# A fifth pair of seven products from the fourth gate/up chunk on, and VectorE's order at the ends of chunks, in a two-layer hybrid encoder

## The chip, the cores and the metric

The kernel runs on one core of one Trainium2 chip. The metric is the device time of one execution in microseconds, as the median of several executions. Profiles show one execution on the chip, with times from the start of its span. TensorE is PE in the profile, VectorE is DVE, ScalarE is ACT, GpSimd is POOL, and SyncE, which issues most DMAs, is SP.

## What is computed

The reference is a trunk of two layers (`DEPTH`) over 256 tokens of width 2048. Everything is float32.

```python
def swiglu(h, w_gate, w_up, w_down):
    return (jax.nn.silu(h @ w_gate) * (h @ w_up)) @ w_down

def reference(x, ...):
    for l in range(DEPTH):
        h = rms_norm(x, pre_mix_norm[l])
        m = hybrid_mixer(h, l, ...)
        x = x + rms_norm(m, post_mix_norm[l])
        h = rms_norm(x, pre_ffn_norm[l])
        f = swiglu(h, w_gate[l], w_up[l], w_down[l])
        x = x + rms_norm(f, post_ffn_norm[l])
    return x
```

The change touches `h @ w_gate` and `h @ w_up` only: 256 x 2048 by 2048 x 5632, twice in each layer.

## The kernel before

**Products.** A float32 product is made of three matmuls on operands rounded to a shorter format: the rounded part `hi` and the rest `lo` of both sides give hi·hi, hi·lo and lo·hi, all added in one PSUM bank (`product`, lines 1075 to 1080). The activations are split once. Each weight block of 256 x 512 (128 partitions x 1024 values) is loaded from HBM into a room `raw`, ScalarE writes `hi` (line 306) and VectorE writes `lo = raw - hi` (line 316). TensorE multiplies a 128 x 128 block of activations by 128 x 512 values in one matmul.

**Chunks and pairs.** The 5632 columns of gate and up are cut into 11 chunks of 512, and the 2048 rows into eight pairs `kp` of two 128-row blocks (loop at line 1253). A chunk adds into four banks, gate and up for each of the two token tiles. One pair takes eight block products, 24 matmuls (`eight`, line 1244), or seven, 21 matmuls, by Winograd's form of Strassen's scheme (`seven_products`, lines 1099 to 1114). `gate_sevens` says which pairs of a chunk are "seven" pairs, and `gate_order` in which order the pairs come.

**What a seven pair costs elsewhere.** Its loads go to rooms `G` (the gate block) and `T` (the up block, to which a DMA of POOL's queue adds half of the gate block, line 258). `mixed_weights` then does, on ScalarE and VectorE: the split of `T` into `hi` and `lo` (lines 279 and 280, 1024 values), a subtraction in `T` (line 289, 512), an addition in `G` (line 290, 1024), and the splits of `T` and `G` into `Th` and `Tl` (512 and 1024). The sums of activations for a pair (`pair_sums`, line 1227, and `token_sums`, line 1082) are made once per layer, at the places (chunk, pair) of `FORM_AT`. Four of the seven products are shared between output blocks: they add up in four extra banks `p1`, `p6`, `p7`, `q5` over all seven pairs of the chunk.

**The end of a chunk.** After the chunk's last seven pair, `shared_part` (line 1116) reads the extra banks: ScalarE copies `p1`, and VectorE makes the four **shared additions** (lines 1120 to 1123). After the chunk's last pair come the **last additions** (lines 1288 and 1291, two each, from the chunk's own banks), the silu on ScalarE (line 1289) and the two multiplications to `act` (line 1293). The banks change sides: the extra banks of chunk c are the main banks of chunk c+1, and the main banks of chunk c are the extra banks of chunk c+1 (lines 1254 and 1275). So TensorE can start chunk c+1 only when the shared additions of chunk c have read the extra banks, and can start the first seven pair of chunk c+1 only when the last additions have read the main banks. The transposes of `act` for the down stage run in the last pair of the next chunk (line 1270).

**Who sets the order.** Each engine works through its own queue in order. Weights are asked for `LOOKAHEAD` = 4 blocks ahead (`feed`, line 296; `fetch`, line 218); there are 4 rooms `raw`, 6 each for `hi` and `lo`, 3 for `G`, 4 for `T`. A scheduler orders the instructions on each engine; `tc.issue_after(i)` puts the instructions inside it behind `i` in their engine's order, and is no wait by itself. `behind()` (line 324) puts the next `held[1]` subtractions of line 316 behind the last shared addition. `helped` (line 207) names gate blocks whose `lo` is made by POOL instead of VectorE (line 309): the second and third pair of each chunk from chunk 2 on; the second one also waits for the latest matmul of a seven pair ("the shared port"). `put_away` (line 362) stores a quarter of x (512 KB, SP's queue) at four chunks of each layer (`AWAY_AT`).

Of the kernel before, what the change touches and what calls it, by code (L numbers as in the profile page):

```python
# [9 lines left out]
F32 = mybir.dt.float32  # L10
# [3 lines left out]
ALU = mybir.AluOpType  # L14
# [10 lines left out]
FF = 5632  # L25
CW = 512
# [18 lines left out]
FIRST_ORDER = (0, 1, 3, 2, 7, 4, 6, 5)  # L45
NEXT_SEVEN = (4, 5, 6)
MORE_SEVEN = (2, 3, 4, 5, 6)
MORE_AT = (2, 3, 4, 5, 6, 7, 8, 9)
MORE_ORDER = (0, 2, 1, 3, 4, 5, 6, 7)
FORM_AT = {(0, 1): 4, (0, 2): 6, (0, 5): 5, (1, 3): 2, (1, 5): 3}  # L50
DOWN_SEVEN = ((4, 7, 10, 12, 15, 17, 20), (3, 5, 8, 10, 13, 15, 18))

AFTER = mybir.DependencyInfo(mybir.DependencyClass.Sync, mybir.DependencyReason.DATA)
# [2 lines left out]
LEVEL = 232  # L56
EARLY = 4
LEAD = 6
AWAY_AT = (1, 3, 4, 5)
X_BACK = 12  # L60


# [4 lines left out]
def gate_sevens(c):  # L67

    if c in MORE_AT:
        return MORE_SEVEN  # L70
    return (FIRST_SEVEN, NEXT_SEVEN)[c] if c < 2 else SEVEN


def gate_order(c):

    if c in MORE_AT:
        return MORE_ORDER
    return FIRST_ORDER if c == 0 else tuple(range(KT // 2))
# [89 lines left out]
def kernel(  # L168
# [15 lines left out]
    nc = tc.nc  # L184
# [14 lines left out]
    def four_banks(odd, names):  # L199
        makers = (bank, bank, bank, last_bank) if odd else (acc_bank,) * 4  # L200
        return [make(n) for make, n in zip(makers, names)]


    order, plan, sevens, plain, own = weight_order()
# [1 line left out]

    helped = {}
    for lay in plan:
        for c in range(2, FF // CW):
            for n in (1, 2):  # L210
                helped[lay["gate"][c, gate_order(c)[n]]] = n == 1
    newest_seven = [None]
# [50 lines left out]
    def mixed_weights(i):  # L263

        g, u = raws[i - 1], raws[i]
        hi = wpool.tile([P, 2, CW], F32R, tag="hi", bufs=6, name=f"hi{i}")
        lo = wpool.tile([P, 2, CW], F32R, tag="lo", bufs=6, name=f"lo{i}")
        if i in own:
            th = wpool.tile([P, 2, CW], F32R, tag="hi", bufs=6, name=f"Th{i}")
            tl = wpool.tile([P, 2, CW], F32R, tag="lo", bufs=6, name=f"Tl{i}")  # L270
            th2 = mix_pool[0].tile([P, 2 * (S + P)], F32R, tag="ah", bufs=1, name=f"T2h{i}")[:, 0:CW]
            tl2 = mix_pool[0].tile([P, 2 * (S + P)], F32R, tag="al", bufs=1, name=f"T2l{i}")[:, 0:CW]
        else:
            th = mix_pool[0].tile([P, 3, CW], F32R, tag="Th", bufs=1 if i in plain else 2, name=f"Th{i}")
            tl = mix_pool[0].tile([P, 3, CW], F32R, tag="Tl", bufs=1 if i in plain else 2, name=f"Tl{i}")
            th2, tl2 = th[:, 2, :], tl[:, 2, :]

        def split(h, l, w):
            nc.scalar.activation(h, w, AF.Copy)  # L279
            nc.vector.tensor_tensor(out=l, in0=w, in1=h.bitcast(F32), op=ALU.subtract)  # L280

        if i in plain or i in own:
            with after_rests():
                nc.vector.tensor_tensor(out=u[:, 0, :], in0=g[:, 0, :], in1=u[:, 0, :], op=ALU.add)
        split(hi, lo, u)
        t1, b22 = ((hi[:, k, :], lo[:, k, :]) for k in range(2))
        t3, t4 = ((th[:, k, :], tl[:, k, :]) for k in range(2))
        t2 = u[:, 1, :]
        nc.vector.tensor_tensor(out=t2, in0=t2, in1=u[:, 0, :], op=ALU.subtract)  # L289
        nc.vector.tensor_tensor(out=g, in0=g, in1=t2.unsqueeze(1).to_broadcast([P, 2, CW]), op=ALU.add)  # L290
        split(th2, tl2, t2)
        split(th[:, 0:2, :], tl[:, 0:2, :], g)
        t2 = th2, tl2
        return {"b22": b22, "t1": t1, "t2": t2, "t3": t3, "t4": t4}
# [25 lines left out]

    rests = []
    held = [None, 0]

    def behind():

        if held[1] == 0:
            return nullcontext()
        held[1] -= 1
        return tc.issue_after(held[0].ins)

    def after_rests():

        return tc.issue_after(rests[-1].ins)
# [28 lines left out]
    def put_away(nm, n):  # L362

        if n == 0:
            away.append(kept.tile([P, NT, D], F32, name=f"away_{nm}"))
        t, h = divmod(n, 2)
        with in_turn():
            nc.sync.dma_start(away[-1][:, t, h * D // 2 : (h + 1) * D // 2], xs[t][h])
# [168 lines left out]
    def start(gen, n=1):  # L537
        running.append([clock[0] + n, gen])
# [577 lines left out]
    def shared_part(extra, w):  # L1116

        p1, p6, p7, q5 = extra
        nc.scalar.copy(w[0], p1)
        nc.vector.tensor_tensor(out=w[1], in0=p6, in1=w[0], op=ALU.subtract)  # L1120
        nc.vector.tensor_tensor(out=w[2], in0=p7, in1=w[1], op=ALU.add)  # L1121
        nc.vector.tensor_tensor(out=w[1], in0=q5, in1=w[1], op=ALU.add)
        return nc.vector.tensor_tensor(out=w[3], in0=q5, in1=w[2], op=ALU.add)

    def shared_sign(t, col):
        return ALU.subtract if (t, col) == (1, 0) else ALU.add

    xT = None
    for l in range(L):
# [27 lines left out]
        for kp in LATE_O:  # L1157
            i, j = (plan[l]["o"][c, kp] for c in (2, 3))
# [4 lines left out]
            if kp == O_SEVEN[0]:  # L1163
                extra = four_banks(False, [f"{q}_o{l}" for q in ("p1", "p6", "p7", "q5")])
# [44 lines left out]
        LAST = FF // CW - 1  # L1209
# [24 lines left out]
        def eight(banks, c, kp, toks, first, last):  # L1234
            g, u = weights(plan[l]["gate"][c, kp], LOOKAHEAD), weights(plan[l]["up"][c, kp], LOOKAHEAD)
            for kk in range(2):
                st = xT[2 * kp + kk]
                for t in toks:
                    tick()
                    stat = (st[:, 0, t * P : (t + 1) * P], st[:, 1, t * P : (t + 1) * P])  # L1240
                    two = banks[2 * t : 2 * t + 2]
                    for part, j, n in ((1, 0, 0), (0, 0, 1), (0, 1, 2)):
                        for a, w in zip(two, (g, u)):
                            nc.tensor.matmul(a, stat[part], w[j][:, kk, :], start=first and kk + n == 0, stop=last and kk == 1 and n == 2)  # L1244
# [8 lines left out]
        for c in range(FF // CW):  # L1253
            banks = four_banks(1 - c % 2, [f"c{q}_{l}_{c}" for q in ("11", "12", "21", "22")])
            mine = gate_sevens(c)
            order = gate_order(c)
            if c == 0:
                for t in range(NT):
                    for kp in order[:2]:
                        eight(banks, c, kp, (t,), kp == order[0], False)  # L1260
                order = order[2:]
            extra = None
            for n, kp in enumerate(order):
                if n == 1 and c in AWAY_AT:
                    put_away(f"ffn{l}", AWAY_AT.index(c))
                if (c, n) in FORM_AT:
                    with after_rests():
                        pair_sums(FORM_AT[c, n])
                if c and n == 7:
                    start(turned(c - 1), 4)  # L1270
                if kp not in mine:
                    eight(banks, c, kp, range(NT), kp == 0, kp == order[-1])
                    continue
                if kp == mine[0]:
                    extra = four_banks(c % 2, [f"{q}_{l}_{c}" for q in ("p1", "p6", "p7", "q5")])
                seven(banks, extra, c, kp, kp == mine[0], kp == mine[-1])
                if kp == mine[-1]:
                    w = [pool.tile([P, CW], F32, tag="t2", name=f"w{j}_{l}_{c}") for j in range(4)]
                    held[:] = shared_part(extra, w), 2
            if c == 0:  # L1280
                act.append(act_room(0))
            if c < LAST:
                act.append(act_room(c + 1))
                results[c] = [act[c + 1].rearrange("p k n -> p (k n)")[:, t * CW : (t + 1) * CW] for t in range(NT)]
            else:
                results[c] = [w[0], w[2]]
            for t in range(NT):
                nc.vector.tensor_tensor(out=w[2 * t], in0=banks[2 * t], in1=w[2 * t], op=shared_sign(t, 0))
                nc.scalar.activation(w[2 * t], w[2 * t], AF.Silu, scale=rs[t][:, 0:1])
            for t in range(NT):  # L1290
                nc.vector.tensor_tensor(out=banks[2 * t + 1], in0=banks[2 * t + 1], in1=w[2 * t + 1], op=ALU.add)
            for t in range(NT):
                nc.vector.scalar_tensor_tensor(
                    out=results[c][t], in0=banks[2 * t + 1], scalar=rs[t][:, 0:1], in1=w[2 * t], op0=ALU.mult, op1=ALU.mult
                )
# [11 lines left out]
        for half in range(2):  # L1307
# [48 lines left out]
            for kp in range(nkp - tail):  # L1356
# [10 lines left out]
                if kp == mine[0]:  # L1367
                    extra = four_banks(1 - half, [f"{q}_d{l}_{half}" for q in ("p1", "p6", "p7", "q5")])
# [90 lines left out]
```

## Time and profile before

| what | value |
|---|---|
| median of 3 runs | 2205.46 us (2204.45 to 2209.45) |
| the profiled execution's own time | 2204.04 us |
| its span, first to last instruction | 2202.3 us |
| mean granted TensorE clock | 0.998 |
| TensorE busy with matmuls | 2175.5 us |
| VectorE busy | 1947.0 us |
| ScalarE busy | 1397.5 us |
| GpSimd busy | 245.7 us |
| gate/up, layer 0 (chunks 0 to 10) | 396.15 to 866.42 us of the span |
| gate/up, layer 1 | 1490.81 to 1962.41 us |

The profile's busy time of TensorE counts a matmul from its start to its modelled end, and matmuls overlap, so 99% busy does not say that TensorE issues at its full rate. The better measure used below is the length of a chunk: each chunk has a fixed number of matmuls, so chunks with the same work can be compared. A view by stretches gives, for each stretch of the span, the busy time of each engine with its number of instructions in brackets. A chunk is cut here at the first matmul of line 1244 into its main banks.

### The profile page before, as it was taken

Reading aid. Unit: us, or ns where it says so; the run is one execution under the profiler, and the core shown is the slowest. Engines: PE = TensorE matmul, PEld = TensorE weight load, DVE = VectorE, ACT = ScalarE, POOL = GpSimd, SP = SyncE. Lnnn points to the kernel's source line nnn. Section 1 sums busy time; section 2 is a strip of 40 time slices with the busy share of each in tenths; the row PEclk is TensorE's granted clock in tenths of the full one; section 3 lists DMA queues with packets and bytes.
Section 4 is the critical chain, followed back from the end, with each engine's and each line's share of the span. In section 5 each row is a group of like instructions: output and inputs, shape, how many; then the busy total and the mean of one; then the engine's idle time right before and its main releaser. Section 6 shows DMA issues by size and latency. Waiting matters only on the chain.

```text
span 2202.3 us, 28747 instructions
## 1 busy us (share of the span) xinstructions
PE 2175.5 (99%) x9944; PEld 1782.5 (81%) x9944; DVE 1947.0 (88%) x2651; ACT 1397.5 (63%) x2087; POOL 245.7 (11%) x239
## 2 busy tenths in 40 slices
PE   9999999999999999999999999999999999999998
PEld 7888888777788888888878888887777888888886
DVE  7888658999999999989878886579999999999997
ACT  7666665765666666666665656657556666566664
POOL 1100000022122120000010000000211211200000
PEclk9999999999999999999999999999999999999999
DMA  9545555587787777767465555556878878767673
GB/s 336 177 163 174 190 195 168 187 279 216 235 256 228 223 236 233 241 211 258 146 239 172 189 174 176 190 171 202 266 215 234 263 225 230 235 227 234 205 262 101
DMA packets 140851, 471.49 MB, mean 214 GB/s; under 512 B 16016, under 2 KB 17040, under 8 KB 140192
## 3 DMA queue, kind: packets, MB, share of 16 engines
q1 hardware_dynamic: 121952, 436.03, 57.5%
q0 software_dynamic: 18176, 33.07, 9.0%
q8 instruction: 78, 1.28, 0.2%
q10 hardware_dynamic: 576, 0.54, 0.1%
q14 instruction: 69, 0.57, 0.1%
HBM read 461.19 MB, written 8.39 MB: 213 GB/s over the span
## 4 chain that ended last, share of the span: by engine, by line
PE 84%; DVE 10%; DMA 2%; issue 2%; ACT 1%; DVEq 0%; SPq 0%; ACTq 0%
PE c L1244 15%; PE in L1078 7%; PE in L1080 7%; PE in L1079 7%; PE dn L1340 4%; PE dn L1341 4%; PE dn L1343 4%; PE p L1079 2%; PE p L1080 2%; PE c L1079 2%; PE c L1080 2%; PE c L1078 2%; PE o L563 2%; PE p L1078 2%; PE o L564 2%
## 5 line engine op out<-in xcount | busy, mean ns | idle before, releaser
L316 DVE TENSOR_TENSOR lo<-raw,hi 128x1024 fp32r<-128x1024 f32 x472 | 568.4, 1227 | 99.2 <-ACT hi L306 97.9
L306 ACT ACTIVATE hi<-raw 128x1024 fp32r<-128x1024 f32 x490 | 505.5, 1054 | 108.7 <-DMA raw<-in_weights_in_turn_dram 37.6
L1244 PE MATMUL c<-hi,xF 128*128 128x512 f32 x1248 | 338.5, 392 | 0.9 <-ACT act L1224 0.5
L258 POOL DMA_DIRECT2D T<-in_weights_in_turn_dram x126 | 110.9, 880 | 1466.3 <-DMA T<-in_weights_in_turn_dram 778.1
L1244 PEld LDWEIGHTS c<-hi,xF 128*128 128x128 f32 x1248 | 231.8, 188 | 50.5 <-DVE w L1121 1.3
L1244 PE MATMUL c<-lo,xF 128*128 128x512 f32 x624 | 193.4, 390 | 2.5 <-DVE lo L316 2.5
L279 ACT ACTIVATE Th<-T 128x512 fp32r<-128x512 f32 x126 | 79.0, 627 | 167.3 <-DVE T L289 149.6
L280 DVE TENSOR_TENSOR lo<-T,hi 128x1024 fp32r<-128x1024 f32 x126 | 172.4, 1368 | 2.9 <-ACT hi L279 2.8
L279 ACT ACTIVATE hi<-T 128x1024 fp32r<-128x1024 f32 x126 | 132.4, 1050 | 66.1 <-PE c L1080 51.9
L1340 PE MATMUL dn<-hi,jh 128*128 128x512 f32 x432 | 168.2, 389 | 0.0
L1341 PE MATMUL dn<-lo,jh 128*128 128x512 f32 x432 | 168.1, 389 | 0.0
L279 ACT ACTIVATE Th<-G 128x1024 fp32r<-128x1024 f32 x126 | 133.3, 1058 | 52.1 <-DVE G L290 51.3
L280 DVE TENSOR_TENSOR Tl<-G,Th 128x1024 fp32r<-128x1024 f32 x126 | 158.8, 1260 | 4.2 <-ACT Th L279 4.2
L306 ACT ACTIVATE hi<-G 128x1024 fp32r<-128x1024 f32 x126 | 133.0, 1056 | 43.0 <-DMA G<-in_weights_in_turn_dram 15.7
L290 DVE TENSOR_TENSOR G<-G,T 128x1024 f32<-128x1024 f32 x126 | 153.8, 1220 | 2.2
L1244 PEld LDWEIGHTS c<-lo,xF 128*128 128x128 f32 x624 | 117.1, 188 | 27.6 <-DVE lo L316 3.0
L316 DVE TENSOR_TENSOR lo<-G,hi 128x1024 fp32r<-128x1024 f32 x108 | 131.5, 1218 | 7.9 <-ACT hi L306 7.6
L1343 PE MATMUL dn<-hi,jl 128*128 128x512 f32 x432 | 133.0, 389 | 0.0
L1078 PE MATMUL in<-hi,xT 128*128 128x512 f32 x328 | 131.8, 404 | 0.6 <-ACT hi L883 0.6
L1078 PE MATMUL in<-hi,xI 128*128 128x512 f32 x328 | 131.1, 401 | 0.0
L1079 PE MATMUL in<-lo,xI 128*128 128x512 f32 x328 | 128.0, 390 | 0.3 <-DVE lo L316 0.3
L1080 PE MATMUL in<-hi,xT 128*128 128x512 f32 x328 | 128.3, 392 | 0.0
(485 smaller groups left out, 4955.8 us busy)
## 6 DMA issues: line engine op xcount, KB each, us to landing
raw<-in_weights_in_turn_dram SPq DMA_DIRECT2D x490, 512.0 KB, 4.6
T<-in_weights_in_turn_dram SPq DMA_DIRECT2D x126, 512.0 KB, 5.2
G<-in_weights_in_turn_dram SPq DMA_DIRECT2D x126, 512.0 KB, 5.5
T<-in_weights_in_turn_dram POOLq DMA_DIRECT2D x126, 256.0 KB, 5.8
GU<-in_weights_in_turn_dram SPq DMA_DIRECT2D x32, 512.0 KB, 6.3
V<-in_weights_in_turn_dram SPq DMA_DIRECT2D x8, 512.0 KB, 3.7
away_ffn<-x SPq DMA_DIRECT2D x8, 512.0 KB, 7.5
xd<-away_ffn SPq DMA_DIRECT2D x8, 512.0 KB, 9.3
```

The lines of the kernel that those rows point to most:

```text
L279: nc.scalar.activation(h, w, AF.Copy)
L280: nc.vector.tensor_tensor(out=l, in0=w, in1=h.bitcast(F32), op=ALU.subtract)
L290: nc.vector.tensor_tensor(out=g, in0=g, in1=t2.unsqueeze(1).to_broadcast([P, 2, CW]), op=ALU.add)
L306: nc.scalar.activation(hi, raw, AF.Copy)
L316: rest = nc.vector.tensor_tensor(out=lo, in0=raw, in1=hi.bitcast(F32), op=ALU.subtract)
L1078: nc.tensor.matmul(a, sh, hi, start=first, stop=False, skip_group_check=open_sums[0])
L1079: nc.tensor.matmul(a, sh, lo, start=False, stop=False, skip_group_check=open_sums[0])
L1080: return nc.tensor.matmul(a, sl, hi, start=False, stop=last, skip_group_check=open_sums[0])
L1244: nc.tensor.matmul(a, stat[part], w[j][:, kk, :], start=first and kk + n == 0, stop=last and kk == 1 and n == 2)
L1340: nc.tensor.matmul(accs[c, t], sh, hi[:, kk, :], start=first, stop=False, skip_group_check=open_sums[0])
L1341: nc.tensor.matmul(accs[c, t], sh, lo[:, kk, :], start=False, stop=False, skip_group_check=open_sums[0])
L1343: nc.tensor.matmul(accs[c, t], sl, hi[:, kk, :], start=False, stop=last, skip_group_check=open_sums[0])
```

## The change

Chunk 2 goes from five seven pairs to the four of the ordinary chunks, in the ordinary order 0 to 7; chunks 3 to 9 keep five. The activations' sums for pair 3 are made in chunk 2 instead of chunk 1 (`FORM_AT`), and the first quarter of x is put away in chunk 2 instead of chunk 1. POOL's help (`helped`) begins in chunk 1. In the ends of chunks whose next chunk has a seven pair as its second pair (chunks 2 to 8), three things are put in a row on VectorE: the shared additions, then the subtractions of that second pair's split, then the last additions. At the other ends only one later `lo` subtraction, not two, is put behind the shared additions (two still at the last chunk).

```diff
-MORE_AT = (2, 3, 4, 5, 6, 7, 8, 9)
+MORE_AT = (3, 4, 5, 6, 7, 8, 9)
 MORE_ORDER = (0, 2, 1, 3, 4, 5, 6, 7)
-FORM_AT = {(0, 1): 4, (0, 2): 6, (0, 5): 5, (1, 3): 2, (1, 5): 3}
+FORM_AT = {(0, 1): 4, (0, 2): 6, (0, 5): 5, (1, 3): 2, (2, 4): 3}
...
-AWAY_AT = (1, 3, 4, 5)
+AWAY_AT = (2, 3, 4, 5)
...
     for lay in plan:
-        for c in range(2, FF // CW):
+        for c in range(1, FF // CW):
             for n in (1, 2):
                 helped[lay["gate"][c, gate_order(c)[n]]] = n == 1
...
         def split(h, l, w):
             nc.scalar.activation(h, w, AF.Copy)
-            nc.vector.tensor_tensor(out=l, in0=w, in1=h.bitcast(F32), op=ALU.subtract)
+            with in_row(i):
+                newest_rest[i] = nc.vector.tensor_tensor(out=l, in0=w, in1=h.bitcast(F32), op=ALU.subtract)
...
+    follows, newest_rest = {}, {}
+
+    def in_row(i):
+
+        return tc.issue_after(follows[i].ins) if i in follows else nullcontext()
...
-                    held[:] = shared_part(extra, w), 2
+                    end = shared_part(extra, w)
+                    second = plan[l]["up"][c + 1, gate_order(c + 1)[1]] if c < LAST else None
+                    if second in sevens:
+                        follows[second] = end
+                    else:
+                        held[:] = end, 2 if second is None else 1
...
+            def ending():
+                return tc.issue_after(newest_rest[second].ins) if second in follows else nullcontext()
+
             for t in range(NT):
-                nc.vector.tensor_tensor(out=w[2 * t], in0=banks[2 * t], in1=w[2 * t], op=shared_sign(t, 0))
+                with ending():
+                    nc.vector.tensor_tensor(out=w[2 * t], in0=banks[2 * t], in1=w[2 * t], op=shared_sign(t, 0))
                 nc.scalar.activation(w[2 * t], w[2 * t], AF.Silu, scale=rs[t][:, 0:1])
             for t in range(NT):
-                nc.vector.tensor_tensor(out=banks[2 * t + 1], in0=banks[2 * t + 1], in1=w[2 * t + 1], op=ALU.add)
+                with ending():
+                    nc.vector.tensor_tensor(out=banks[2 * t + 1], in0=banks[2 * t + 1], in1=w[2 * t + 1], op=ALU.add)
```

## The prediction

> **What bounds the kernel now.** I read the page first, then the view by stretches cut at the chunks, then TensorE's waits, then VectorE's and POOL's timelines at the chunk ends where TensorE waits.
>
> ```profile
> span 2202.3 us, 28747 instructions
> PE 2175.5 (99%) x9944; PEld 1782.5 (81%) x9944; DVE 1947.0 (88%) x2651; ACT 1397.5 (63%) x2087; POOL 245.7 (11%) x239
> ```
>
> TensorE looks full, but its matmuls overlap, so what it loses has to be read from the lengths of chunks. Columns: stretch, length, then busy time and count by engine.
>
> ```profile
> core 0: us, PE busy (x) PEld busy (x) DVE busy (x) ACT busy (x) POOL busy (x), PEclk, DMA share, GB/s
> 442.18:486.02 43.84, 43.14 (x192) 34.85 (x190) 42.53 (x59) 25.12 (x30) 8.99 (x6) 1.00 0.92 299
> 486.02:530.73 44.71, 42.96 (x186) 33.67 (x186) 44.24 (x46) 25.99 (x30) 10.59 (x7) 1.00 0.69 207
> 530.73:575.19 44.46, 42.20 (x186) 33.74 (x185) 43.93 (x47) 27.75 (x34) 9.33 (x8) 1.00 0.82 247
> 575.19:618.01 42.82, 41.60 (x187) 33.98 (x185) 42.72 (x46) 26.47 (x31) 9.10 (x7) 1.00 0.78 235
> 618.01:660.00 41.99, 41.34 (x187) 33.98 (x186) 41.73 (x45) 27.73 (x34) 9.15 (x7) 1.00 0.83 248
> ...
> 701.07:742.62 41.55, 41.31 (x187) 33.97 (x186) 40.31 (x45) 26.85 (x32) 9.17 (x7) 1.00 0.81 232
> 742.62:783.64 41.02, 41.02 (x186) 33.99 (x185) 40.56 (x45) 26.61 (x32) 9.21 (x7) 1.00 0.80 230
> ...
> 824.72:866.42 41.70, 41.70 (x190) 34.61 (x189) 40.38 (x44) 27.14 (x35) 4.17 (x3) 1.00 0.62 199
> ...
> 1536.85:1580.84 43.99, 43.19 (x192) 34.84 (x190) 42.53 (x59) 25.03 (x30) 8.99 (x6) 1.00 0.90 295
> 1580.84:1628.48 47.64, 44.64 (x185) 34.81 (x186) 45.60 (x48) 27.07 (x32) 9.62 (x7) 0.96 0.71 210
> 1628.48:1671.50 43.02, 41.94 (x187) 33.82 (x186) 42.33 (x45) 26.69 (x32) 9.41 (x8) 1.00 0.81 239
> 1671.50:1714.35 42.85, 41.62 (x186) 33.98 (x185) 42.75 (x46) 26.48 (x31) 9.02 (x7) 1.00 0.81 238
> 1714.35:1756.33 41.98, 41.33 (x187) 33.98 (x185) 41.72 (x45) 27.71 (x34) 9.70 (x8) 1.00 0.82 250
> ```
>
> These are chunks 1 to 5, 7, 8 and 10 of layer 0, and 1 to 5 of layer 1. Chunk 8, five seven pairs, takes 41.02 with no idle; chunk 10, four, takes 41.70. The three matmuls between them make 0.68, so a matmul is 0.227, and a chunk of three seven pairs would take 42.38. Against these floors chunks 1 to 5 and 7 lose 1.46, 3.69, 3.44, 1.80, 0.97 and 0.53 in layer 0 (11.9), and 1.61, 6.62, 2.00, 1.83 and 0.96 in layer 1 (13.0; its chunk 7 lost nothing). **24.9 us** are lost, beside a VectorE that is busy 43.93 of 44.46. Who ends the waits (layer 0, chunks 1 to 10):
>
> ```profile
> PE p L1079 <- DVE Tl L280: 2.3, 5, 0.8
> PE q L1078 <- DVE act L1293: 1.5, 1, 1.5
> PE p L1078 <- DVE act L1293: 0.9, 1, 0.9
> ```
>
> Idle here starts at a matmul's modelled end, so it is less than the loss. VectorE's splits are late for the last seven pairs, and its last additions free the banks late for the next chunk's first. At the end of chunk 1, VectorE and POOL:
>
> ```profile
> 482.55 2.81 DVE L280 TENSOR_TENSOR lo<-T,hi 128x1024 fp32r<-128x1024 f32 x1
> ...
> 488.82 2.89 DVE L280 TENSOR_TENSOR Tl<-T,Th 128x512 fp32r<-128x512 f32 x1
> ...
> 495.16 1.39 DVE L1293 SCALAR_TENSOR_TENSOR act<-c,rs_ffn,w 128x512 f32<-128x512 f32 x2
> ...
> 479.62 4.67 POOL L309 TENSOR_TENSOR lo<-G,hi 128x1024 fp32r<-128x1024 f32 x1 [3.88 <-ACT ss L1095]
> ...
> 488.33 2.83 POOL L309 TENSOR_TENSOR lo<-raw,hi 128x1024 fp32r<-128x1024 f32 x1 [0.35 <-ACT hi L306]
> ```
>
> And at the end of chunk 6, where nothing is lost:
>
> ```profile
> 693.20 1.22 DVE L316 TENSOR_TENSOR lo<-raw,hi 128x1024 fp32r<-128x1024 f32 x1
> 694.33 0.68 DVE L1120 TENSOR_TENSOR w<-p,w 128x512 f32<-128x512 f32 x1
> ...
> 696.38 0.68 DVE L1123 TENSOR_TENSOR w<-q,w 128x512 f32<-128x512 f32 x1
> 696.98 1.63 DVE L280 TENSOR_TENSOR lo<-T,hi 128x1024 fp32r<-128x1024 f32 x1
> ...
> 706.05 1.36 DVE L316 TENSOR_TENSOR lo<-raw,hi 128x1024 fp32r<-128x1024 f32 x1
> ...
> 695.11 2.41 POOL L309 TENSOR_TENSOR lo<-G,hi 128x1024 fp32r<-128x1024 f32 x1 [4.93 <-PE c L1080]
> ```
>
> From start to start a VectorE instruction of 1024 values holds its queue for 1.13 (693.20 to 694.33), one of 512 for 0.60 (696.38 to 696.98). At 482.55 a subtraction took 1.6 more and at 488.82 one took 2.2 more, each until POOL's subtraction ended. The additions that read PSUM run beside POOL's 2.41 at their usual 0.68. So where the four shared additions stand together, POOL's subtraction is nearly free (1.63 instead of 1.22); where a split stands among them, VectorE is held.
>
> The Trainium skill ("SBUF — State Buffer", section "SBUF: two separate sides") says that VectorE instructions with two SBUF inputs and GpSimd's exclude each other for a whole instruction. These rows agree; by that rule the two subtractions newly given to POOL may cost VectorE more than they save, which is the second rival.
>
> **The change part by part.** *Chunk 2, five to four seven pairs.* TensorE gets three matmuls more in each layer: 6 x 0.227 = **+1.36**. VectorE's queue loses 4 x 1.13 + 2 x 0.60 = 5.7 and gets 2 x 1.13 = 2.3.
>
> *Pair 3's sums move from chunk 1 to 2; two `lo` of chunk 1 go to POOL.*
>
> ```profile
> L1231 DVE TENSOR_TENSOR f<-xF 128x256 f32<-128x256 f32 x2 | 0.8, 419 | 0.0
> L1096 DVE TENSOR_TENSOR ss<-s,ss 128x512 fp32r<-128x512 f32 x1 | 0.7, 686 | 0.0
> L1087 DVE TENSOR_TENSOR s<-f 128x128 f32<-128x128 f32 x1 | 0.3, 289 | 0.0
> ```
>
> Two, one and four such instructions, less 0.08 of overlap each, hold VectorE 2.1. Chunk 1's queue gets shorter by 2.1 + 2 x 1.13 = 4.4. POOL's two subtractions there come beside shared and last additions of chunk 0; between 0 and 2 x 2.4 of blocking, I take 0.6. Chunk 1's loss was 1.5; I leave 0.3, because ScalarE's splits wait for `hi` rooms that TensorE frees, so VectorE can't run far ahead.
>
> What queues behind POOL's new work and behind the moved store:
>
> ```profile
> 440.87 0.86 POOL L258 DMA_DIRECT2D T<-in_weights_in_turn_dram  x1 [26.47 <-DMA T<-in_weights_in_turn_dram]
> 453.75 1.04 ACT L279 ACTIVATE hi<-T 128x1024 fp32r<-128x1024 f32 x1
> 450.37 1.06 ACT L306 ACTIVATE hi<-raw 128x1024 fp32r<-128x1024 f32 x1 [3.39 <-DMA raw<-in_weights_in_turn_dram]
> ...
> T<-in_weights_in_turn_dram POOLq DMA_DIRECT2D x126, 256.0 KB, 5.8
> away_ffn<-x SPq DMA_DIRECT2D x8, 512.0 KB, 7.5
> ```
>
> POOL's next DMA would land by 440.87 + 0.86 + 5.8 = 447.5 and is used at 453.75: 6.2 of room for 2.4 of subtraction, so nothing. The store leaves SP's queue ahead of the load that ScalarE waits for at 450.37, and stands in chunk 2, where the DMA share is 0.69 instead of 0.92. I cost it at nothing; uncovered, one landing of 7.5 delayed once a layer is its upper end.
>
> *Chunk 2's losses (3.69 and 6.62).* From one set of shared additions to the next, VectorE's new order holds 4 shared additions (2.4), one `lo` (1.13), the last additions and multiplications (3.75), then 21 of 1.13, 8 of 0.60 and the sums (2.1): 38.0, against TensorE's 41.70; in the old chunk 2 it was busy 44.24. The first seven pair now comes after two eight pairs, 48 matmuls or 10.9, instead of 5.4, so the wait on the last additions' multiplications (0.9) goes. In layer 1 the long wait goes, and with it a slow stretch:
>
> ```profile
> 1612.85 0.50 PE L1079 MATMUL p<-Tl,sh 128*128 128x512 f32 x1 [1.66 <-DVE Tl L280]
> 1614.14:1617.55 3.41, 3.41 (x10) 2.62 (x9) 3.41 (x5) 2.61 (x4) 0.72 (x1) 0.50 0.82 264
> ```
>
> After 1.66 of idle the granted clock was 0.50 for 3.41: eight matmuls at 0.427, 1.6 lost. The Trainium skill ("TensorE: Matmul & The Clock Gate", section "What's actually happening") has the clock fall only after about 3.4 us of idle. The row shows a shorter idle ahead of it, so I let the 1.6 go with the wait; if by that rule it isn't this wait's, the gain is 1.6 less. I leave 0.6 in each layer, for the last `Tl` of the chunk, which by the tally comes just when it is needed.
>
> *The ends of chunks 2 to 8, in a row.* The order adds no wait by itself, but whatever holds the split now holds the last additions, and behind them ScalarE's silu, the multiplications, and TensorE's products in `q5`. The same instructions took 706.05 − 694.33 = 11.7 at the end of chunk 6, and the order within does not make them longer. `q5` is wanted 30 matmuls into the next chunk, 701.07 + 6.8 = 707.9: 1.8 of room. At chunk 3, 1.53 of waiting for `q5` goes, because VectorE is no longer behind nor held by POOL. From then on a chunk has the instructions that kept VectorE busy 40.56 of 41.02 in chunk 8: it keeps up. TensorE's own order changes too: in the last two seven pairs of chunks 4 to 9 the second matmul of `p7` moves from place 11 of 21 to places 16 and 18, 5 or 7 x 0.227 = 1.1 or 1.6 later, which covers the 0.8 wait on `Tl`. I leave 0.6 in chunk 3 and 0.5 in chunks 4 to 9.
>
> **Sum.** Lost 24.9; left 2 x (0.3 + 0.6 + 0.6 + 0.5) = 4.0; matmuls 1.36. Gain 24.9 − 4.0 − 1.36 = 19.5. The profiled execution took 2204.04, 1.7 beyond its span; 2204.0 − 19.5 = 2184.5. The median of the runs is 1.4 above that execution: **2186.0**. The best possible is 2205.5 − 24.9 + 1.4 = 2182.
>
> **Rivals.**
> 1. *Half of it.* VectorE stays late at the ends of chunks 2 and 3, since the five-seven chunks give it only 0.5 to spare. For: its busy 41.73 of 41.99 in chunk 5. Against: the 3.7 to spare in chunk 2. Half of 24.9 stays: 2205.5 − 12.4 + 1.4 = 2194.
> 2. *POOL's lock costs what it saves.* POOL's two new subtractions in each layer block VectorE for 2.4 where they save 1.13, and those at the ends of chunks 1 and 2 block it as in the rows at 482.55 and 488.82. Chunk 1 then keeps its 1.5; chunks 2 and 3 get 1.6 + 2.2 less from VectorE each, with 3.7 and 0.5 to spare, so some 3.4 is lost; and the later chunks keep their 2.9. Left: 2 x 7.8 = 15.6, and 2205.5 − 9.3 + 1.4 = 2198. For: the two rows. Against: the shared additions now stand together.
> 3. *Not what it says.* The waits only move: VectorE's total is the bound, 2202 to 2206.
> 4. *Slower.* In the new row, POOL's subtraction starts only when the shared additions are over. Then the split is held 2.4 instead of 0.4, the last additions pass the 1.8 of room, and `q5` is late at the ends of chunks 2 to 8, 14 times. A second subtraction that also hits a split adds 2.2 (the 488.82 row): 14 x (2.0 + 2.2 − 1.8) = 34 against 23.5: 2216. It decides from 1.7 of waiting per end on. Against: POOL waits for the same pair's last matmul that frees the shared additions.
>
> **How the numbers follow.** Forecast 0.60 (2182 to 2190); rivals 1 and 2 together 0.26 (2190 to 2200); 3, 0.06; 4, 0.08. The range runs from 2181 to 2198, which leaves out about 0.17. A measurement of this kernel tells about 0.2%, 4.4 us, from no change: faster 0.86, same 0.06, slower 0.08.
>
> **What would show it.** Right: chunks 1, 2 and 3 at 42.4 to 42.7, 41.7 to 42.3 and 41.0 to 41.7, no granted clock under 1 in layer 1, POOL's first subtraction beside four shared additions, and no wait of TensorE for the multiplications to `act`. Wrong: a chunk 3 to 9 above 42; VectorE instructions of 1024 values near 2.8 at the new ends; ScalarE's `hi<-T` waiting for a DMA in chunk 1.

## The result and the profile after

The changed kernel takes **2188.97 us** (median, 2188.84 to 2191.47) against 2205.63 us before (2201.71 to 2209.45): a ratio of 0.9927, 95% interval 0.9914 to 0.9940, or 16.7 us less. The forecast was 2186.0, with 2181 to 2198 as its range. The page of the changed kernel begins:

```profile
span 2187.3 us, 28757 instructions
...
PE 2170.0 (99%) x9950; PEld 1782.2 (81%) x9950; DVE 1914.1 (88%) x2639; ACT 1393.4 (64%) x2083; POOL 251.1 (11%) x241
```

VectorE works 33 us less, and TensorE has the six matmuls more. Where the time came from is in the view by stretches, cut at the chunks as before: here chunks 1, 2, 3, 4, 7 and 9 of layer 0, and 1, 2, 3 and 6 of layer 1.

```profile
440.86:483.70 42.84, 42.70 (x192) 35.10 (x191) 40.10 (x54) 25.44 (x31) 9.01 (x7) 1.00 0.87 293
483.70:525.84 42.14, 42.14 (x190) 34.46 (x189) 41.39 (x48) 25.73 (x32) 10.10 (x8) 1.00 0.87 270
525.84:567.53 41.69, 41.34 (x186) 33.97 (x185) 40.10 (x45) 26.76 (x32) 9.05 (x7) 1.00 0.79 229
567.53:608.88 41.35, 41.35 (x186) 33.97 (x185) 40.06 (x45) 26.80 (x32) 8.80 (x8) 1.00 0.82 246
...
691.35:732.92 41.57, 41.35 (x186) 33.97 (x185) 40.07 (x45) 26.86 (x32) 9.19 (x7) 1.00 0.80 234
...
774.38:817.07 42.69, 41.64 (x187) 33.89 (x185) 39.03 (x45) 26.84 (x32) 8.07 (x6) 1.00 0.65 202
...
1529.26:1572.62 43.36, 42.77 (x193) 35.02 (x191) 40.53 (x54) 25.18 (x31) 9.18 (x7) 1.00 0.85 290
1572.62:1614.75 42.13, 42.13 (x189) 34.46 (x188) 41.15 (x48) 25.73 (x32) 10.05 (x8) 1.00 0.86 263
1614.75:1656.12 41.37, 41.34 (x186) 33.97 (x185) 40.01 (x45) 26.70 (x32) 8.55 (x7) 1.00 0.82 238
...
1739.29:1781.20 41.91, 41.34 (x187) 33.97 (x185) 40.03 (x45) 26.97 (x32) 9.25 (x7) 1.00 0.80 233
```

Against the floors of 42.38, 41.70 and 41.02, chunks 1, 2 and 3 now lose 0.46, 0.44 and 0.67 in layer 0 (before: 1.46, 3.69 and 3.44), and 0.98, 0.43 and 0.35 in layer 1 (before: 1.61, 6.62 and 2.00). Chunks 4 to 9 together lose 3.42 and 3.40, where 1.0 for both layers was forecast. VectorE is not the busy one there: 40.06 of 41.35 in chunk 4. Before, the same six chunks lost 3.41 and 3.09 in all, so the later chunks together gained nothing. Chunk 9 of layer 0, at 42.69, is above 42, which the prediction named as a sign of being wrong, and chunk 1, at 42.84 and 43.36, is above the 42.7 that it named for being right. The waits of TensorE in chunks 1 to 10, first of layer 0, then of layer 1:

```profile
PE p L1085 <- DVE Tl L281: 1.3, 3, 0.7
PE p L1084 <- ACT Th L279: 0.3, 1, 0.3
...
PE p L1085 <- DVE Tl L281: 2.2, 5, 0.6
```

The waits for the last additions are gone; a wait for the split `Tl` is left.

### The profile page after: what moved, and what is told of

It reads as the page before. It is cut to its first block, busy times and chain, and to the rows that moved or that the text cites. A ratio compares the mean times of both kernels' runs of the same rounds, so it can differ in the third digit from the quotient of the medians.

```text
span 2187.3 us, 28757 instructions
## 1 busy us (share of the span) xinstructions
PE 2170.0 (99%) x9950; PEld 1782.2 (81%) x9950; DVE 1914.1 (88%) x2639; ACT 1393.4 (64%) x2083; POOL 251.1 (11%) x241
## 3 DMA queue, kind: packets, MB, share of 16 engines
q8 instruction: 78, 1.28, 0.2%
## 4 chain that ended last, share of the span: by engine, by line
PE 87%; DVE 7%; issue 2%; DMA 2%; ACT 1%; SPq 0%; DVEq 0%; ACTq 0%
PE c L1250 16%; PE in L1084 7%; PE in L1086 7%; PE in L1085 7%; PE dn L1356 4%; PE dn L1357 4%; PE dn L1359 4%; PE p L1085 2%; PE c L1086 2%; PE c L1084 2%; PE c L1085 2%; PE p L1086 2%; PE p L1084 2%; PE o L569 2%; PE o L570 2%
## 5 line engine op out<-in xcount | busy, mean ns | idle before, releaser
L1250 PE MATMUL c<-hi,xF 128*128 128x512 f32 x1280 | 346.0, 391 | 0.1
L1250 PEld LDWEIGHTS c<-hi,xF 128*128 128x128 f32 x1280 | 238.3, 188 | 49.1 <-DVE xF L493 0.6
L1250 PE MATMUL c<-lo,xF 128*128 128x512 f32 x640 | 198.2, 390 | 2.5 <-DVE lo L317 2.5
L281 DVE TENSOR_TENSOR Tl<-G,Th 128x1024 fp32r<-128x1024 f32 x124 | 151.2, 1220 | 14.5 <-ACT Th L279 14.5
L281 DVE TENSOR_TENSOR lo<-T,hi 128x1024 fp32r<-128x1024 f32 x124 | 156.5, 1262 | 2.9 <-ACT hi L279 2.4
L1084 PE MATMUL in<-hi,xT 128*128 128x512 f32 x328 | 131.4, 402 | 0.5 <-ACT hi L889 0.5
L1084 PE MATMUL in<-hi,xI 128*128 128x512 f32 x328 | 131.1, 401 | 0.0
L1086 PE MATMUL in<-hi,xI 128*128 128x512 f32 x328 | 127.9, 391 | 0.0
```

What stands on the lines that cost most here:

```text
L281: newest_rest[i] = nc.vector.tensor_tensor(out=l, in0=w, in1=h.bitcast(F32), op=ALU.subtract)
L1084: nc.tensor.matmul(a, sh, hi, start=first, stop=False, skip_group_check=open_sums[0])
L1086: return nc.tensor.matmul(a, sl, hi, start=False, stop=last, skip_group_check=open_sums[0])
```

## The experiments

Each edit is written against the changed kernel. They ran in three groups, each beside the kernel before, whose median was 2204.93, 2204.66 and 2204.89 us, so the times can be compared with each other and with 2188.97. "The row" is the order at the chunk ends. Its first half puts the second pair's subtractions behind the shared additions; its second half puts the last additions behind those subtractions.

**The order alone.**

```diff
-MORE_AT = (3, 4, 5, 6, 7, 8, 9)
+MORE_AT = (2, 3, 4, 5, 6, 7, 8, 9)
-FORM_AT = {..., (2, 4): 3}
+FORM_AT = {..., (1, 5): 3}
-AWAY_AT = (2, 3, 4, 5)
+AWAY_AT = (1, 3, 4, 5)
-        for c in range(1, FF // CW):
+        for c in range(2, FF // CW):
```

> The changed kernel with only its order kept: chunk 2 has five seven pairs again, pair 3's sums stand in chunk 1 again, the halves are put away from chunk 1 on, and the lo of chunk 1 are made by VectorE; the row at the chunk ends stays. Theory (VectorE carries a lag from chunks 1 and 2, and the row by itself frees no time): chunk 2 loses its 3 to 7 us as before, the row takes away only the 1.5 of waiting for q5 in chunk 3 and a part of the split that POOL holds; 2200 to 2204. Rival (the row is what brings the gain): within 2 us of the changed kernel, 2187 to 2191. Rival (the row is late for q5 when VectorE is behind): above 2206.

Measured: 2222.71 us, ratio to before 1.0079 (1.0065 to 1.0093). The order alone is 18 us slower than the kernel before, so my 2200 to 2204 missed, and the second part of the fourth rival is there to be seen: POOL's second subtraction meets a split. The first one still lies beside the shared additions. At the end of chunk 6, VectorE, then POOL:

```profile
706.40 1.23 DVE L291 TENSOR_TENSOR G<-G,T 128x1024 f32<-128x1024 f32 x1
708.19 2.68 DVE L281 TENSOR_TENSOR Tl<-T,Th 128x512 fp32r<-128x512 f32 x1 [0.56 <-ACT Th L279]
710.79 1.21 DVE L281 TENSOR_TENSOR Tl<-G,Th 128x1024 fp32r<-128x1024 f32 x1
711.93 1.27 DVE L1303 TENSOR_TENSOR w<-c,w 128x512 f32<-128x512 f32 x2
...
707.78 2.53 POOL L310 TENSOR_TENSOR lo<-raw,hi 128x1024 fp32r<-128x1024 f32 x1
```

A subtraction of 0.68 lasts 2.68, until POOL's second one ends at 710.31, and the last additions stand behind it. Chunks 1 to 10 of layer 0 then show who is late:

```profile
PE p L1084 <- DVE w L1303: 5.9, 4, 2.5
PE p L1084 <- ACT Th L279: 5.0, 8, 1.1
PE q L1084 <- DVE act L1309: 2.3, 3, 0.8
```

**All but the order.**

```diff
-                    if second in sevens:
-                        follows[second] = end
-                    else:
-                        held[:] = end, 2 if second is None else 1
+                    held[:] = end, 2
```

> The changed kernel without the row at the chunk ends: one held count of 2 at every chunk end, as before, all else as changed. Theory (lag): chunk 2 still has its slack, so VectorE comes to the ends of chunks 2 and 3 in time, and only the split between the shared additions that POOL holds (about 2 us at an end) comes back where there is little to spare; 2190 to 2194, with chunk 2 within 0.5 of 42.1. Rival (the row is what brings the gain): 2198 to 2204, with waits of TensorE for the last additions' products at the start of each of chunks 3 to 5. Rival (the row costs something in the late chunks, which now lose 3.4 a layer): below 2188, with chunks 5 to 9 back at 41.02 to 41.3.

Measured: 2182.62 us, ratio 0.9897 (0.9884 to 0.9911), the third expectation: without the row the kernel is 6.3 us faster than with it. The next two runs say which half costs.

**The first half of the row alone.**

```diff
-                return tc.issue_after(newest_rest[second].ins) if second in follows else nullcontext()
+                return nullcontext()
```

> The changed kernel with the first half of the row alone: the split subtractions of the second pair's up block follow the shared additions and one lo is held behind these; the last additions are free again. Theory (the row's cost comes from the last additions standing behind the Tl from G, whose Th ScalarE makes only after the act copies that wait 4.6 for TensorE's transposes): the cost goes, 2181 to 2185, chunks 4 to 9 at 41.0 to 41.3, ScalarE's wait for the transposes no longer ahead of Th. Rival (the split that must follow the shared additions is what costs): 2187 to 2190, as the changed kernel.

**The second half alone.**

```diff
-        return tc.issue_after(follows[i].ins) if i in follows else nullcontext()
+        return nullcontext()
```

> The changed kernel with the second half of the row alone: the last additions stand behind the last split subtraction of the second pair's up block; that block's splits are free to go where the scheduler puts them. Theory (this half is what costs): 2187 to 2191, chunks 4 to 9 losing 3 to 4 a layer, ScalarE's waits of 4 to 5 for the transposes and VectorE's of 0.7 for Th at the chunk ends. Rival (the first half is what costs): 2181 to 2185.

Measured: **2181.65 us** with the first half (0.9896, 0.9882 to 0.9909), **2202.90 us** with the second (0.9994, 0.9985 to 1.0003). The first half is nearly free by itself (2181.65 beside 2182.62, and the runs of the two overlap); the second costs 20 alone and 7.3 behind the first half. I had not expected more than 2191 of it. One thing more differs in the second half alone: no later subtractions are put behind the shared additions by `held` at the row's ends, as they are in "all but the order", so nothing keeps the split from among them. The 20 us are the price of the second half and of that together. With the first half alone, chunks 3 and 9 of layer 0 stand at the floor:

```profile
526.22:567.24 41.02, 41.02 (x186) 34.05 (x185) 40.85 (x45) 26.67 (x32) 8.51 (x6) 1.00 0.77 228
...
772.42:813.44 41.02, 41.02 (x186) 34.05 (x185) 39.11 (x45) 27.00 (x33) 8.30 (x6) 1.00 0.65 203
```

What the second half does is seen at one end, that of chunk 5. VectorE in the changed kernel:

```profile
649.74 0.69 DVE L281 TENSOR_TENSOR Tl<-T,Th 128x512 fp32r<-128x512 f32 x1
651.18 1.23 DVE L281 TENSOR_TENSOR Tl<-G,Th 128x1024 fp32r<-128x1024 f32 x1 [0.74 <-ACT Th L279]
652.32 1.28 DVE L1303 TENSOR_TENSOR w<-c,w 128x512 f32<-128x512 f32 x2
```

And with the first half alone:

```profile
648.79 0.68 DVE L281 TENSOR_TENSOR Tl<-T,Th 128x512 fp32r<-128x512 f32 x1
649.39 0.68 DVE L1303 TENSOR_TENSOR w<-c,w 128x512 f32<-128x512 f32 x1
649.99 0.69 DVE L1307 TENSOR_TENSOR c<-c,w 128x512 f32<-128x512 f32 x1
650.59 1.22 DVE L281 TENSOR_TENSOR Tl<-G,Th 128x1024 fp32r<-128x1024 f32 x1
```

`Tl<-G` needs the `Th` that ScalarE makes from `G`. When the last additions are free, two of them fill the time in which ScalarE works; when they must follow, VectorE stands still for 0.74. In chunks 3 to 9 of layer 0 it does so 7 times, 5.2 us in all:

```profile
DVE Tl L281 <- ACT Th L279: 5.2, 7, 0.7
```

That row is of the changed kernel; with the first half alone there is none. How the 0.74 reaches TensorE is read from the rows of one wait, that for `Tl<-G` in chunk 7 of layer 0, which starts at 691.35 (690.33 with the first half alone). VectorE in the changed kernel:

```profile
717.89 1.22 DVE L317 TENSOR_TENSOR lo<-raw,hi 128x1024 fp32r<-128x1024 f32 x1
719.02 1.21 DVE L281 TENSOR_TENSOR Tl<-G,Th 128x1024 fp32r<-128x1024 f32 x1
```

And with the first half alone:

```profile
715.90 1.22 DVE L281 TENSOR_TENSOR Tl<-G,Th 128x1024 fp32r<-128x1024 f32 x1
```

A `lo` of 1.13 now stands ahead of this `Tl`, and VectorE comes to the two 26.5 us into the chunk instead of 25.6 into it, 1.0 later. TensorE's matmul is late by 0.4. That VectorE is 1.0 behind because it stood still for 0.74 at the end of the chunk is argued; no run moves one without the other. A full VectorE alone isn't the reason: with the first half alone it is busy 40.85 of 41.02 in chunk 3, and nothing is lost. Half of layer 0's 3.42 lies in chunk 9 (1.67), where ScalarE waits 3.18 for a late `G`; over chunks 3 to 9 it waits six times for one, 11.7 us in all, against 2.0. With the second half alone POOL comes in as well. VectorE, then POOL, at the same end:

```profile
648.67 2.67 DVE L281 TENSOR_TENSOR lo<-T,hi 128x1024 fp32r<-128x1024 f32 x1
651.26 0.68 DVE L1128 TENSOR_TENSOR w<-q,w 128x512 f32<-128x512 f32 x1
...
647.86 2.40 POOL L310 TENSOR_TENSOR lo<-G,hi 128x1024 fp32r<-128x1024 f32 x1 [4.69 <-PE c L1086]
```

The split stands among the shared additions again and is held until POOL ends at 650.26. The first half exists to avoid this.

**The whole row with later transposes.** A test of a theory for the 0.74: that ScalarE's copies of the transposes make `Th` late.

```diff
-                    start(turned(c - 1), 4)
+                    start(turned(c - 1), 6)
```

> The changed kernel with its whole row, but the transposes of the chunk before start 6 instead of 4 half-pairs on, so that ScalarE's copies of them stand behind the second pair's Th in its order. Theory (the row costs because the last additions stand behind a Tl from G whose Th ScalarE makes late, once the act copies are done): VectorE's wait of 0.7 at the ends goes; 2182 to 2186. Rival (the wait for Th is not the act copies' doing, the last additions simply no longer fill the time in which ScalarE makes Th from G): 2187 to 2190, and VectorE still waits for Th at the ends.

Measured: 2213.14 us, 1.0040 (1.0027 to 1.0053). Neither expectation held in its time. The copies stood behind `Th`, VectorE waited 0.68 for it all the same, and POOL's second subtraction, which now started inside the row (VectorE, then POOL), made it worse:

```profile
655.79 2.55 DVE L281 TENSOR_TENSOR Tl<-T,Th 128x512 fp32r<-128x512 f32 x1 [0.68 <-ACT Th L279]
...
655.38 2.41 POOL L310 TENSOR_TENSOR lo<-raw,hi 128x1024 fp32r<-128x1024 f32 x1 [1.04 <-ACT hi L307]
```

So moving the copies does not take the wait away. That they have no part in it is not shown: ScalarE has another split in their place here, and the wait shown is for the `Th` from `T`. The eight pair has four steps, so a start at 6 puts the transposes into the next chunk's first pair; TensorE also waited for the copies themselves (2.9 us in chunks 1 to 10 of layer 0, some 6.7 us into a chunk), so not all of this run's 24 us are the row's.

**Chunk 2 alone.** The row goes as in "all but the order", `FORM_AT`, `AWAY_AT` and `helped` as in "the order alone"; only chunk 2's four seven pairs stay.

> The kernel before with one part of the change: chunk 2 has four seven pairs in the plain order. Pair 3's sums stay in chunk 1, the store and POOL's help stay where they were, and there is no row. Theory (VectorE's lag is made in chunks 1 and 2; chunk 2 lightened by 3.4 takes up chunk 1's lag late): chunk 1 loses 1.5 as before, chunk 2 up to 1, chunks 3 on at most 0.5 each; 2184 to 2190. Rival (the parts work only together, since chunk 1's 4.4 are carried into chunk 2): 2193 to 2200.

Measured: 2188.47 us, 0.9925 (0.9912 to 0.9937), a time as expected, though not the losses: chunk 3 still loses 2.3 and 4.1, where at most 0.5 was expected. One line brings 16.2 us, as much as the whole change; the other parts with the first half of the row bring some 7 more, and its second half takes them back. The parts don't simply add, as the next runs show.

**Five seven pairs in chunk 2, with the first half of the row.** The first half alone, with `MORE_AT`, `FORM_AT` and `AWAY_AT` as in "the order alone"; POOL still helps in chunk 1.

> The version with the first half of the row alone (2181.65), with five seven pairs in chunk 2 as before (pair 3's sums then stand in chunk 1 and the halves are put away from chunk 1 on); POOL helps in chunk 1. Theory (chunk 2's load is what VectorE has no time for): chunk 2 or 3 loses 2 to 5 a layer, and with 0.3 of slack a chunk the lag lasts to chunk 5; 2189 to 2198. Rival (the help in chunk 1 and the kept order were enough): 2180 to 2183, as 1.36 of matmuls goes.

**Sums in chunk 1, with the first half of the row.** The same with `MORE_AT` as changed: pair 3's sums and the first store in chunk 1.

> The version with the first half of the row alone (2181.65), with pair 3's sums in chunk 1 and the halves put away from chunk 1 on, as before. Theory (late VectorE in chunk 1, but then slack in chunk 2): chunk 1 as 42.4 to 43.3 and 2181 to 2184, chunks 3 on at 41.02 to 41.3. Rival (the move of the sums is worth the 6 us that it was worth beside the whole row, 2195.0 against 2189.0): 2186 to 2189.

**Sums in chunk 1, with the whole row.** `FORM_AT` and `AWAY_AT` as in "the order alone", all else as changed.

> The changed kernel with pair 3's sums back in chunk 1 and the halves put away from chunk 1 on; chunk 2 keeps four seven pairs, and row and help stay. Theory: VectorE has 2.1 more in chunk 1 and 2.1 less in chunk 2, which has the slack; chunk 1 loses some 0.5 to 1.5 more a layer and chunk 2 nothing less; 2190 to 2192. Rival (chunk 1 is limited by its loads, whose share of the DMA engines is 0.87, and by the store): the difference shows as waits of ScalarE for loads in chunk 1, not as VectorE's. Rival (moving the sums is of no weight): 2188 to 2190.

Measured: 2195.66 us with five (0.9957, 0.9944 to 0.9969), 2190.84 with four and the sums in chunk 1 (0.9934, 0.9921 to 0.9946), and 2195.03 with those under the whole row (0.9956, 0.9944 to 0.9969). With five the time is as expected (2189 to 2198); half the row and the help bring 9.2 there (2195.66 against 2204.89), while with four and the sums in chunk 1 they bring nothing (2190.84 beside the 2188.47 of "chunk 2 alone", which ran in another group). With the sums in chunk 1, chunk 2's lighter load is worth 4.8; the sums and the store, which moved together, are worth 9.2 beside half the row and 6.1 beside the whole. Neither expectation held for the other two: the rival's 2186 to 2189 was nearer to 2190.84 than my 2181 to 2184, and 2195.03 is above both 2190 to 2192 and 2188 to 2190. The loss is not in chunk 1, where I looked for it, but in chunks 2 and 3 (3.24 in chunk 3 of layer 0 with half the row). Layer 0 with half a row, first chunks 1 to 3 with the sums in chunk 1, then chunks 1 and 2 with the sums in chunk 2 (its chunk 3 is shown above):

```profile
441.07:484.55 43.48, 42.73 (x193) 35.11 (x191) 40.50 (x59) 23.24 (x28) 7.82 (x6) 1.00 0.74 250
484.55:527.88 43.33, 42.04 (x190) 34.52 (x188) 38.42 (x41) 27.38 (x32) 9.93 (x9) 1.00 0.92 296
527.88:572.14 44.26, 41.81 (x186) 33.83 (x185) 42.63 (x46) 27.27 (x32) 9.24 (x7) 1.00 0.71 210
```

```profile
441.26:484.10 42.84, 42.68 (x193) 35.11 (x192) 40.51 (x54) 25.28 (x31) 9.17 (x7) 1.00 0.87 292
484.10:526.22 42.12, 42.12 (x189) 34.47 (x188) 41.78 (x49) 25.70 (x32) 10.03 (x8) 1.00 0.87 271
```

VectorE does no more in chunk 1, and less in chunk 2 (38.42). What moves is the loads: the DMA share is 0.74 and 0.92 instead of 0.87 and 0.87. The rows say where the loads stop. In chunk 1, VectorE, then SyncE, with the sums in chunk 1:

```profile
475.63 1.22 DVE L317 TENSOR_TENSOR lo<-raw,hi 128x1024 fp32r<-128x1024 f32 x1
...
476.92 0.33 SPq L241 DMA_DIRECT2D raw<-in_weights_in_turn_dram  x1
```

And with the sums in chunk 2:

```profile
468.78 1.22 DVE L317 TENSOR_TENSOR lo<-raw,hi 128x1024 fp32r<-128x1024 f32 x1
...
470.03 0.33 SPq L241 DMA_DIRECT2D raw<-in_weights_in_turn_dram  x1
```

A room `raw` is free when its `lo` is made. With the sums in chunk 1 this `lo` stands behind them and behind the next pair's work in VectorE's order, 6.9 later, and SyncE issues no load from 462.97 to 476.92. At the end of chunk 2, with the sums in chunk 1, VectorE, then POOL:

```profile
528.89 1.23 DVE L291 TENSOR_TENSOR G<-G,T 128x1024 f32<-128x1024 f32 x1 [3.85 <-POOL lo L310]
...
525.57 0.86 POOL L258 DMA_DIRECT2D T<-in_weights_in_turn_dram  x1 [10.32 <-PE c L1250]
526.13 2.72 POOL L310 TENSOR_TENSOR lo<-G,hi 128x1024 fp32r<-128x1024 f32 x1
```

VectorE adds to `G` in place, so it must wait until POOL has read `G`; POOL's subtraction stands behind an accumulating DMA, which adds to a `T` and needs that `T` loaded. (The profile names a TensorE instruction as what ended its idle time; nothing in the code ties the two.) With the sums in chunk 2 the same subtraction starts at 520.26, 0.7 after the first shared addition and ahead of the accumulating DMA, and no such wait appears. The late `G` goes on to ScalarE's `Th` (530.14, after 3.31 of waiting), to the copy of a transpose behind that, and to TensorE's first products of chunk 3:

```profile
531.73 0.96 PE L1250 MATMUL c<-hi,xF 128*128 128x512 f32 x3 [2.10 <-ACT act L1230]
```

So the rows point to the place of the sums in VectorE's order, not to the time that they take; no run moves the sums without the store. That the `T` was late because the DMA engines were full in chunk 2 is argued from the two shares: it landed 8.3 after its issue instead of 5.6. In "chunk 2 alone", which has the sums in chunk 1 too, the same addition waits 2.82 for POOL.

**POOL's help, where it begins and whether at all.** Three kernels: help from chunk 2 on under the whole row and under the first half, and, without the row, no help at all.

```diff
-        for c in range(1, FF // CW):
+        for c in range(2, FF // CW):
```

> The changed kernel with POOL's lo from chunk 2 on, as before, so that VectorE makes all splits of chunk 1; all else as changed. Theory (VectorE's load in chunk 1 is what is late): chunk 1 loses 0.5 to 1 more in each layer; 2190 to 2192. Rival (POOL's two subtractions cost in blocking what they save): no difference or faster, 2187 to 2189, chunk 1 at most 42.9.

> The version with the first half of the row alone (2181.65), with POOL's lo from chunk 2 on as before, so VectorE makes all splits of chunk 1. Theory (VectorE's queue of chunk 1 is what is late, 2.26 more there): chunk 1 loses 0.3 to 1 more in a layer, chunks 3 on nothing; 2182.5 to 2184. Rival (POOL's two subtractions there cost in holding VectorE what they save): 2181 to 2182.

> The changed kernel without the row and with no lo made by POOL: VectorE makes all of them. Theory (POOL's subtraction takes 1.13 from VectorE's queue and gives back 0.2 to 0.5 by holding it): VectorE gets 1.7 more in a chunk where it has 0.3 to spare beside TensorE's 41.02, so chunks 3 to 9 take 42.2 to 42.7; 2198 to 2208. Rival (the two exclude each other so much that the help costs what it saves): 2181 to 2187, chunks 3 to 9 at 41.0 to 41.4.

Measured: 2191.18 us (0.9935, 0.9923 to 0.9947), 2183.98 (0.9904, 0.9889 to 0.9919) and 2200.57 (0.9981, 0.9973 to 0.9990), each in the range of the theory, though single chunks are off: the kernel without help has chunks 3 and 4 at 41.45 to 41.65, where 42.2 to 42.7 was expected. In that one `range(0)` stands in the edited line, and the row is taken out as in "all but the order". The help in chunk 1 is worth 2.2 and 2.3 us, with chunk 1 at 44.20 and 44.22 instead of 42.84 and 43.39 under the first half. All 40 of POOL's subtractions are worth 2200.57 − 2182.62 = 18.0, or 0.45 each. Without help chunk 7 of layer 0 takes 42.89:

```profile
694.81:737.70 42.89, 42.62 (x187) 33.42 (x186) 41.59 (x47) 26.30 (x32) 4.35 (x5) 1.00 0.77 232
```

## Why the prediction was right, and where it was not

**The lag of chunks 1 to 3 was the cost, and it went.** Of their losses of 8.6 in layer 0 and 10.2 in layer 1, 1.6 and 1.8 are left; I had left 1.5 in each. Chunk 2 alone shows that lightening it is enough to bring as much as the whole change; chunk 3, which still loses 2.3 and 4.1 there, comes to 0.67 and 0.35 with the other parts. The waits for the last additions' multiplications went, as said.

**The six matmuls** are there (9950 instructions of TensorE on the page instead of 9944), and chunk 2 ends 0.4 above its new floor, where 0.6 had been left.

**The sums and the store** I counted as 2.1 of VectorE's time in chunk 1. Their worth of 6 to 9 us is real, but it lies in chunks 2 and 3, and it comes by the loads that stop in chunk 1 and by POOL's queue, as far as the rows show. The sum has no term for that.

**The step that failed is "the order adds no wait by itself".** I asked what might hold the split in the row, and not what VectorE would do while it waits for ScalarE in the middle of it. Before, the last additions could fill that time. The term "0.5 in chunks 4 to 9", 1.0 for both layers, measured 3.42 + 3.40 = 6.8, and 0.1 a layer with the last additions set free. The 1.8 of room for `q5` was not the point: `q5` was never late in the changed kernel. Where TensorE waits in chunks 4 to 9, it is mostly some 28.6 us into the chunk, for the `Tl` of the fourth of its five seven pairs. Its matmul did move from place 11 to 16 of 21, 1.1 later, as forecast; but VectorE's order moved too, by a `lo` of 1.13 ahead of that `Tl` in chunks 4, 5, 7 and 8 of layer 0, and the two cancel. So TensorE's own order does not cover the wait, as I had argued, except where little is lost (0.11 in chunk 6 of layer 0, 0.07 in chunk 9 of layer 1). That the lost 0.74 leads to this wait is argued from the rows; that the free last additions take it away is shown.

**The sum.** Left were 10.2 instead of 4.0. The 24.9 had left out 0.4 of small losses in chunks 6, 8 and 9, so the stage gained 24.9 + 0.4 − 10.2 − 1.4 = 13.7, not 19.5. That the time came so near the forecast is due to what I did not claim: 1.3 ahead of the stage, which begins at 394.82 instead of 396.15 (in the other runs between 394.95 and 396.51, with the same code before it), and 1.7 by which the medians differ more than the profiled spans (16.7 against 15.0). That was luck. The mechanism was right; the stage's gain came out at seven tenths of its size.

**The rivals.** *Half of it* had the wrong place: the ends of chunks 2 and 3 are not late. *POOL's lock* is real in single rows and still worth less than the help. *Slower* described what the order does when POOL's second subtraction meets the row, and the order alone showed it, 18 us slower. It did not decide in the changed kernel: there, at the end of chunk 5, VectorE is early and POOL starts its second subtraction (652.24) when the splits of the row are over.

**A better version** is the change with the first half of the row only: 2181.65, 23 us under the kernel before of its group (0.9896, 0.9882 to 0.9909) and 7.3 under the changed one, with chunks 3 to 9 at 41.02 to 41.06. What it still loses is 0.5 and 1.0 in chunk 1 and 0.4 in chunk 2.

## What to carry to other kernels

Before an engine's order is fixed by hand, look in that order for an instruction that waits for another engine, and for what fills the wait now: work that may go anywhere is what hides it. An engine that is nearly full gains most where its peak is cut, and one chunk made lighter was worth more here than an order fixed at the end of every chunk. An order fixed for a part of the instructions also moves the rest: look at where the scheduler then puts them. Test the parts of a change apart, since a part that costs 7 us can hide in a whole that gains 17.

## What the runs showed of the hardware

**The half clock.** In chunk 3 of layer 1, the kernel with chunk 2 alone and the one with the sums in chunk 1 under the whole row both have an idle of 2.21 on TensorE. Of the first, the matmuls after it and the stretch that follows:

```profile
1617.76 1.62 PE L1250 MATMUL c<-hi,xF 128*128 128x512 f32 x3 [2.21 <-ACT act L1230]
...
1618.32:1621.44 3.12, 3.12 (x9) 2.47 (x8) 3.12 (x5) 2.51 (x4) 2.04 (x1) 0.53 0.74 260
```

Of the second:

```profile
1623.14 0.96 PE L1250 MATMUL c<-hi,xF 128*128 128x512 f32 x3 [2.21 <-ACT act L1230]
...
1623.14:1626.50 3.36, 3.36 (x15) 2.79 (x16) 3.36 (x6) 3.08 (x4) 2.32 (x1) 1.00 0.82 256
```

The same idle brought a clock of 0.53 for 3.1 us once and none the other time. Of the idles of 1.6 and longer in the gate/up stage, over all runs, the clock fell after those of 1.66, 2.21, 2.42, 2.51 and 2.61, and not after 2.21, 2.10, 2.08, 2.03, 1.89 and 1.76. So a wait of some 2 us costs either its own length or 1.6 more. The Trainium skill ("TensorE: Matmul & The Clock Gate", section "What's actually happening") puts the fall after an idle window of about 3.4 us; the falls here come after shorter idles, and the length of the idle alone does not decide. The prediction's 1.6 went with its wait, as assumed.

**POOL beside VectorE.** In the rows shown, a VectorE subtraction of two SBUF inputs that meets POOL's lasts 2.55 to 2.89 instead of 0.68 to 1.22, until POOL's ends. The Trainium skill ("SBUF — State Buffer", section "SBUF: two separate sides") says that two such instructions exclude each other for the whole of the one that starts first, and the trace agrees. Even so, POOL's help was worth 0.45 us for each subtraction. The lock costs where it meets a split; at the end of chunk 5 of the changed kernel POOL's two subtractions (from 644.25 and 652.24) lie beside the shared and the last additions, which read PSUM and keep to their 0.69, or 1.28 for two.
